# Three transposes of a head in front of the low value products, the shared key's part behind the first pooling projection, and the gains on ACT's queue

## The chip, the cores and the metric

The kernel runs on one core of one Trainium2 chip. The metric is the device time of one execution in microseconds, median of several runs. A core has TensorE (PE: matrix products; PEld is its loading of weights, which overlaps products), VectorE (DVE), ScalarE (ACT), GpSimd (POOL), SyncE (SP, which here only issues DMA transfers) and 16 DMA engines. Products land in PSUM and are taken from there by ACT or VectorE.

## The reference

Two layers of a hybrid trunk over 512 tokens with 16 meta tokens in front (528 columns), model width 1024, everything in float32:

```python
h = rmsnorm(h_res, norm_gain[l])
proj = h @ w_in[l]
u_pool, z_pool, c_q, c_kv, k_rope, z_mla, g_pool, g_mla = jnp.split(proj, IN_SPLIT_POINTS, axis=-1)
y_pool = (pool_mix(u_pool, pool_w_group[l], pool_scale[l]) * jax.nn.silu(z_pool)) @ pool_w_up[l]
o_mla = mla(c_q, c_kv, k_rope, pos, ...)
y_mla = (o_mla * jax.nn.silu(z_mla)) @ mla_w_up[l]
merged = jax.nn.sigmoid(g_pool) * y_pool + jax.nn.sigmoid(g_mla) * y_mla
h_res = h_res + merged @ w_out[l]
```

`pool_mix` is, in four channel groups, a mean over the last 2, 4, 8 or 16 tokens less the token itself, times a 128x128 matrix. `mla` is latent attention with 8 heads: queries from c_q, keys of 64 columns a head and values from c_kv, one rotary key of 32 columns shared by all heads (`k_rope`), RMS norms on queries and keys, causal softmax, values of 64 columns a head. The meta tokens are dropped from the output.

## The kernel before, in words

**Products in three parts.** A float32 product is made of three products in a faster 32-bit format: each operand is split in a high part (ACT copies it in that format, `whi`, `hh`, `th`, `kh`) and a low part (VectorE subtracts the high part, `wlo`, `hl`, `tl`, `kl`), and `mm3` (lines 179 to 182) adds high x high, high x low and low x high. Weights are loaded from memory by SP into `raw` (three buffers), split by `wload` (lines 169 to 177, three buffers), and used.

**The stream.** All weight projections of both layers stand in one list, `plan`: c_q, then for m = 0 to 3 a pooling projection u and a key projection k, the value projection v (`v_body`), the pooling gate and the grouped matrix, the queries, the wide gates and the projections out. A generator, `stream`, issues them product by product; `step`, `fill_now(ns)` and `upto(name)` take as much of it as wanted. The attention is written by hand around it: between its pieces `gap()` takes some 2.9 us of the stream, by a planner's estimate. A scheduler then moves instructions a little on each engine; an engine runs its own in order. `behind(ins, other)` (line 274) makes one instruction wait for another; `newest[0]` is the newest `mm3` product, so that `behind(x, newest[0])` keeps x from its engine's queue until TensorE is there.

**The start.** ACT issues the load of the first weight tile, SP the load of the gains (line 122), x's first block (123), the second weight tile and x's second block. `other_loads` (line 140) issues the rest of x behind the gains' landing. Eight warm-up products on a tile of ones (line 136) run first. `split_h` (line 328) splits x times its gain: high part on ACT, low part on VectorE, the first block in two halves.

**Norms and the shared key.** `norm_sums` sums squares for the two RMS norms and, with `kr_sums`, the shared rotary key (`kp`); the reciprocal roots go through memory and come back as `inv` and `cinv`. `kr_rest` (lines 470 to 480) finishes the shared key in two halves: times `inv` on VectorE (474), a copy on POOL (475), a square and a scaled copy on ACT (477, 479), and `rope`: a shuffle and a product on VectorE (529, 530), a product and a sum on POOL (531, 532). In `go` both halves stand behind `up("u1")`. After them come `columns(1)` (norm factors by token for the values, two small loads on SP), and for groups 0 and 1 `window` (sums on POOL, line 563) and `mix` (VectorE lines 570, 573, 574, then the split, 271 on ACT and 272 on VectorE). u is emptied from PSUM by VectorE (line 540), k by VectorE (628). After c_q's last part `k_factors` (lines 515 to 524) makes the reciprocal roots of the key norms on VectorE (519, then `newton`, 279 to 285), stores them and loads them back spread over all partitions for the first heads (`spread_k`, line 733).

**A head.** `head` makes the scores of four query blocks, their maxima, exponentials and sums; POOL scales the probabilities. `pv` multiplies with the values, for the head before: for each key block j = 0 to 3 it transposes the probability blocks i = j to 3 on TensorE into one PSUM tile (line 839: weights are the probabilities, 128 columns are streamed; 4, 3, 2 and 1 transposes, ten a head), splits the tile into `th` and `tl`, and adds two products to the head's output `o`: high part (line 844, 128 weight columns: value high and low part side by side) and low part (line 845, 64 weight columns). Blocks 0 and 1 stand in the middle of the next head's scores, `pv(prev, (0, 1))` (line 800); 2 and 3 behind the next head's keys and queries, `prep` (line 1066). Behind blocks 0 and 1 of an odd head the probabilities of the meta tokens are transposed (line 850). For the last head, after the loop, o lies in one of the score tiles.

Of the kernel before, what the change touches and what calls it, by code (L numbers as in the profile page):

```python
# [9 lines left out]
F32 = mybir.dt.float32  # L10
F32R = mybir.dt.float32r
# [3 lines left out]
ALU = mybir.AluOpType  # L15
# [39 lines left out]
LAG = 2000.0  # L55
SPL = 240
RET = 12500.0
WARM = 8


def cut(v, bits):
# [10 lines left out]
def trunk(ctx, tc, xT, xrow, mrow, pos, win, wkr, wqb, wkb, wvb, wgr, wpu, wmu, wout, gains, const, yT):  # L72
# [17 lines left out]
    def slot(tag, dt=F32, bufs=1, w=W):  # L90
        return sl.tile([P, w], dt, tag=tag, name=nm(tag), bufs=bufs)
# [27 lines left out]

    early.append(slot("rinv"))  # L120
    act.dma_start(early[0][:, 0:512], win[0, MT_CKV, :, 0:512])
    first = sp.dma_start(gn, gains)
# [43 lines left out]

    loads = [0]

    def wload(src, n, spare):
# [5 lines left out]
        act.activation(hi[:, :n], raw[:, :n], AF.Copy)  # L175
        dve.tensor_sub(lo[:, :n], raw[:, :n], hi[:, :n].bitcast(F32))  # L176
        return hi, lo

    def mm3(out, wh, wl, xh, xl, start, stop):
# [85 lines left out]
    def fill_now(ns):  # L265
        end = clk[0] + ns
        while clk[0] < end and step():
            pass

    def split(hi, lo, src, a, b):  # L270
        act.activation(hi[:, a:b], src, AF.Copy)  # L271
        dve.tensor_sub(lo[:, a:b], src, hi[:, a:b].bitcast(F32))  # L272

    def behind(ins, other):
        tc.add_manual_dep(ins.ins, other.ins.name,
# [33 lines left out]
    class Layer:  # L309
        def __init__(self, l):  # L310
            self.l, self.last = l, l == DEPTH - 1
            self.XS = XTOK if self.last else FULL
            self.x0 = NM if self.last else 0
            self.xt = xt if l == 0 else [None] * 8
            self.hs, self.us, self.zps = hbuf, [None] * 4, [None] * 4
            self.cs, self.cqs, self.ys, self.am = [None] * 2, [None] * 6, [None] * 4, [None] * 8
            self.kn, self.qn, self.zms, self.ogs = [None] * 4, [None] * 4, [None] * 4, [None] * 4
            self.qr, self.qf = [None] * 2, [None] * 2
            self.gms, self.mg, self.xr, self.vw = [None] * 8, [None] * 8, [None] * 8, []
            self.made = [None] * 8  # L320
# [4 lines left out]
        def g(self, c):  # L325
            return gn[:, self.l * N_GAIN + c:self.l * N_GAIN + c + 1]

        def split_h(self, k):
            gk, x = self.g(G_H + k), self.xt[k]
            hh, hl = self.hs[k]  # L330
            for a, b in FULL if (self.l, k) == (0, 0) else [(0, T)]:
                made = act.activation(hh[:, a:b], x[:, a:b], AF.Copy, scale=gk)
                self.made[k] = self.made[k] or made
                dve.scalar_tensor_tensor(out=hl[:, a:b], in0=x[:, a:b], scalar=gk, in1=hh[:, a:b].bitcast(F32),
                                         op0=ALU.mult, op1=ALU.subtract)

        def square_x(self, k):
            self.xsq[k] = slot(f"cq{4 + k}" if k < 4 else f"q{k}")
# [176 lines left out]
        def k_factors(self):  # L515
            flat = lambda d: d.rearrange("h (s c) -> (h s) c", c=T // 16)
            na, ny, nt = (sm.tile([P, T // 16], F32, tag=t, name=nm(t)) for t in ("ka", "ky", "kt"))
            sp.dma_start(na, flat(ksr[self.l]))
            dve.tensor_scalar(na, na, 1.0 / QK, EPS, op0=ALU.mult, op1=ALU.add)
            newton(ny, na, nt)  # L520
            sp.dma_start(flat(kdr[self.l]), ny)
            self.bcs = {}
            for h in range(2):
                self.spread_k(h)
# [234 lines left out]
        def head(self, h, kq, prev):  # L759
# [37 lines left out]
            expo(1, 1, s1, pt[1])  # L797
            expo(2, 2, s2, pt[2])
            self.gap()
            self.pv(prev, (0, 1))  # L800
            self.gap()
            sc = sct()
            s0, s4 = sc[:, 0:144], sc[:, 144:144 + T - SPL]
# [19 lines left out]
        def pv(self, prev, js):  # L823
# [11 lines left out]
            for j in js:  # L835
                n = SEQ - P * j
                tr = mmt()
                for i in range(j, 4):
                    pe.transpose(tr[:, P * (i - j):P * (i - j + 1)], pt[i][:, NM + P * j:NM + P * (j + 1)], ident)  # L839
                th = tp.tile([P, W], F32R, tag="th", name=nm("th"), bufs=2)  # L840
                tl = tp.tile([P, W], F32R, tag="tl", name=nm("tl"), bufs=2)
                split(th, tl, tr[:, :n], 0, n)
                out = ops[:, P * j:512]
                pe.matmul(out, vt[:, j, h, :], th[:, :n], start=j == 0, stop=j == 3)  # L844
                pe.matmul(out[0:64], vt[:, j, h, 0:64], tl[:, :n], start=False, stop=j == 3, skip_group_check=True)  # L845
            if js[-1] != 3:
                if odd == 1:
                    tr = sct() if h == H - 1 else mmt()
                    for i in range(4):
                        pe.matmul(tr[0:64, P * i:P * (i + 1)], self.pmr[:, i].rearrange("p a b -> p (a b)"), identr,  # L850
                                  start=True, stop=True)
                    self.mt = slot("racc", F32R)
                    act.activation(self.mt[0:64, 0:512], tr[0:64, :], AF.Copy)
                    act.activation(self.mt[64:96, 0:512], tr[0:32, :], AF.Copy)
                return
            if odd == 0:
                self.op = tmp()
# [159 lines left out]
        def go(self, nxt):  # L1017
            l = self.l
            up = lambda name: upto((l, name))
            if l == 0:  # L1020
                for k in range(8):
                    if k in (0, 1, 3, 5):
                        step()
                    self.split_h(k)
                    if k == 0:
                        other_loads(first)
# [42 lines left out]
            self.pv(prev, (0, 1))  # L1069
            if not self.last:  # L1070
                self.meta_queries()
            fill_now(2600)
# [88 lines left out]
```

## Time and profile before

| | us |
|---|---|
| median of 3 runs | 783.15 (782.77 to 783.66) |
| the profiled execution | 781.26 |
| its span, first to last instruction | 779.4 |
| TensorE busy | 773.6 (99%) |
| VectorE busy | 535.8 (69%) |
| ACT busy | 413.3 (53%) |
| POOL busy | 205.7 (26%) |

A row of the timeline has the start from the span's start and the duration, both in us, then engine, line, operation, tiles written and read, shapes and count; in brackets the idle time of the engine before it, with what ended it. For a product `128*128 128x264` is rows by weight columns, then what is streamed. In a list of groups the last fields are busy time in us, mean of one in ns, and the engine's idle time ahead of these instructions with what ended it. The row of a stretch gives its ends, its length, then for PE, PEld, DVE, ACT and POOL busy time and count, the granted clock of TensorE, the share of the DMA engines' time and GB/s. The record of a product begins while the one before it still drains, so durations overlap, and starts are compared instead.

### The profile page before, as it was taken

What the parts mean: (1) busy time and instruction counts of PE and PEld (TensorE: products, weight loads), DVE (VectorE), ACT (ScalarE), POOL (GpSimd) and SP (SyncE); (2) the same over time, 40 slices, a digit from 0 to 9 for tenths busy, and PEclk for the clock granted to TensorE, in tenths of its full rate; (3) what the DMA queues carried; (4) which work ended last, traced back from release to release, by engine and by line L of the source; (5) the groups of instructions that cost most, each with busy time, mean ns of one, the idle gap of its engine ahead of it and who ended that gap; (6) DMA issues with size and microseconds to landing.
All of it is one profiled execution on the core that took longest, in us unless ns stands there. A gap on an engine that the chain in (4) does not pass through costs nothing.

```text
span 779.4 us, 14530 instructions
## 1 busy us (share of the span) xinstructions
PE 773.6 (99%) x5251; PEld 703.7 (90%) x5251; DVE 535.8 (69%) x1155; ACT 413.3 (53%) x930; POOL 205.7 (26%) x265
## 2 busy tenths in 40 slices
PE   9999999999999999999999999999999999999998
PEld 9999799999999999999997898887788888888887
DVE  5587788357788977685466467774477888755932
ACT  6754655545565665633354456555445666654420
POOL 1024504012333342043130245130132433420500
PEclk9999999999999999999999999999999999999999
DMA  8533233423222212325642322434242322222372
GB/s 282 164 114 92 74 121 103 116 86 100 91 87 88 82 55 79 95 80 150 186 143 83 109 83 89 132 88 142 69 130 88 96 86 85 62 81 68 106 232 95
DMA packets 54931, 84.04 MB, mean 108 GB/s; under 512 B 10006, under 2 KB 18582, under 8 KB 54860
## 3 DMA queue, kind: packets, MB, share of 16 engines
q1 hardware_dynamic: 54716, 82.86, 34.5%
q8 instruction: 41, 0.67, 0.3%
q14 instruction: 30, 0.25, 0.1%
q10 hardware_dynamic: 144, 0.26, 0.1%
HBM read 76.68 MB, written 4.29 MB: 104 GB/s over the span
## 4 chain that ended last, share of the span: by engine, by line
PE 95%; DVE 2%; ACT 1%; issue 1%; DMA 1%; SPq 0%; DVEq 0%; ACTq 0%
PE mm L180 28%; PE mm L182 27%; PE mm L181 27%; PE mm L839 2%; PE S L180 2%; PE S L181 2%; PE S L182 2%; PE o L844 1%; PE o L845 1%; PE S L498 1%; DVE wlo L176 1%; PE S L462 0%; DMA xb<-xT 0%; DVE tmp L570 0%; PE mm L868 0%
## 5 line engine op out<-in xcount | busy, mean ns | idle before, releaser
L180 PE MATMUL mm<-hh,whi 128*128 128x264 f32 (+2 forms) x1096 | 345.5, 317 | 0.2 <-DVE ky L285 0.2
L181 PE MATMUL mm<-hl,whi 128*128 128x264 f32 (+2 forms) x1096 | 343.2, 314 | 0.0
L182 PE MATMUL mm<-hh,wlo 128*128 128x264 f32 (+2 forms) x1096 | 342.5, 315 | 0.0
L176 DVE TENSOR_TENSOR wlo<-raw,whi 128x512 fp32r<-128x512 f32 (+2 forms) x251 | 185.1, 740 | 107.8 <-ACT whi L175 101.5
L175 ACT ACTIVATE whi<-raw 128x512 fp32r<-128x512 f32 (+2 forms) x251 | 150.5, 602 | 178.5 <-PE mm L181 134.7
L180 PEld LDWEIGHTS mm<-hh,whi 128*128 128x128 f32 x1096 | 205.5, 188 | 13.8 <-issue 0.8
L181 PEld LDWEIGHTS mm<-hl,whi 128*128 128x128 f32 x1096 | 206.1, 188 | 12.0
L182 PEld LDWEIGHTS mm<-hh,wlo 128*128 128x128 f32 x1096 | 205.2, 188 | 12.3
L743 POOL TENSOR_TENSOR tmp<-kp,bc 64x528 f32<-64x528 f32 x16 | 24.8, 1553 | 103.6 <-issue 88.4
L818 POOL TENSOR_TENSOR pm<-pa,rs 128x16 f32<-128x16 f32 x32 | 11.2, 351 | 148.5 <-DVE rs L813 148.5
L604 POOL TENSOR_TENSOR racc<-racc,tmp 128x264 f32<-128x264 f32 (+1 forms) x15 | 14.3, 952 | 112.9 <-ACT tmp L603 112.9
L928 POOL TENSOR_TENSOR tmp<-tmp,xb 128x264 f32<-128x264 f32 (+1 forms) x24 | 26.7, 1134 | 57.7 <-DVE tmp L926 55.5
L774 DVE CUSTOM_DVE_ANT_0 S<-S,maskw,nqs 128x272 f32<-128x272 f32 (+4 forms) x80 | 38.5, 498 | 2.3 <-PE S L182 1.9
L180 PE MATMUL mm<-u,whi 128*128 128x264 f32 (+1 forms) x108 | 35.1, 325 | 0.0
L182 PE MATMUL mm<-u,wlo 128*128 128x264 f32 (+1 forms) x108 | 34.7, 321 | 0.0
L180 PE MATMUL mm<-cq,whi 128*128 128x264 f32 (+1 forms) x108 | 34.6, 320 | 0.0
L182 PE MATMUL mm<-cq,wlo 128*128 128x264 f32 (+1 forms) x108 | 34.5, 321 | 0.0
L181 PE MATMUL mm<-cq,whi 128*128 128x264 f32 (+1 forms) x108 | 34.5, 321 | 0.0
L272 DVE TENSOR_TENSOR tl<-mm,th 128x512 fp32r<-128x512 f32 (+1 forms) x64 | 29.3, 482 | 6.8 <-ACT th L271 5.7
L781 ACT ACTIVATE cq<-S,bia 128x400 f32<-128x400 f32 (+2 forms) x48 | 24.5, 515 | 17.8 <-DVE bia L808 8.8
L820 POOL TENSOR_TENSOR cq<-cq,rs 128x384 f32<-128x384 f32 (+1 forms) x32 | 33.5, 1047 | 0.0
L271 ACT ACTIVATE th<-mm 128x512 fp32r<-128x512 f32 (+1 forms) x64 | 25.4, 434 | 6.5 <-PE mm L839 5.9
(271 smaller groups left out, 1370.9 us busy)
## 6 DMA issues: line engine op xcount, KB each, us to landing
raw<-win SPq DMA_DIRECT2D x143, 256.0 KB, 2.6
raw<-wout SPq DMA_DIRECT2D x32, 256.0 KB, 3.1
bc<-kdr SPq DMA_DIRECT2D x16, 264.0 KB, 3.3
raw<-wpu SPq DMA_DIRECT2D x16, 256.0 KB, 2.7
raw<-wmu SPq DMA_DIRECT2D x16, 256.0 KB, 2.7
raw<-wqb SPq DMA_DIRECT2D x12, 256.0 KB, 2.9
xb<-xT SPq DMA_DIRECT2D x8, 264.0 KB, 4.5
tmp<-xT SPq DMA_DIRECT2D x16, 132.0 KB, 3.0
```

What stands on the lines that cost most here:

```text
L175: act.activation(hi[:, :n], raw[:, :n], AF.Copy)
L176: dve.tensor_sub(lo[:, :n], raw[:, :n], hi[:, :n].bitcast(F32))
L180: pe.matmul(out, wh, xh, start=start, stop=False)
L181: pe.matmul(out, wh, xl, start=False, stop=False)
L182: newest[0] = pe.matmul(out, wl, xh, start=False, stop=stop)
L271: act.activation(hi[:, a:b], src, AF.Copy)
L272: dve.tensor_sub(lo[:, a:b], src, hi[:, a:b].bitcast(F32))
L743: gp.tensor_mul(kf[r0:r0 + 64, :], self.kp[r0:r0 + 64, :], bc[r0:r0 + 64, :])]
L774: dve.tensor_tensor_reduce(out=sv, in0=sv, in1=mask, scale=nqs[:, i, h:h + 1], scalar=3e38, op0=ALU.add, op1=ALU.min, accum_out=bia[:, c:c ...
L781: act.activation(pv, sv, AF.Exp, scale=-1.0, bias=bia[:, i:i + 1], accum_out=rs[:, c:c + 1])
L820: gp.tensor_mul(pt[i][:, NM:], pt[i][:, NM:], rs[:, i:i + 1].to_broadcast([P, n - NM]))
L928: gp.tensor_add(t[:, :b - a], t[:, :b - a], self.am[m][:, a:b])
```

## The change

- **Transposes.** `pv` is called three times for a head: with (0,) where (0, 1) stood, with (1,) a gap after the scores' end, ahead of `prep`, and with (2, 3) one gap later. (0,) makes only the seven transposes of blocks 0 and 1 and splits them. (1,) makes the products of blocks 0 and 1: the first product waits for its split's low part, then come a transpose of block 2, half of the low product (256 columns), the other transpose of block 2, the other half; then block 1's first product, block 3's transpose, and block 1's low product. Blocks 2 and 3 share one PSUM tile and one split of 384 columns. (2, 3) makes their products. An order-only dependency (`follow`) keeps each triple together. For the last head, after the loop, all three transposes stand together ahead of the products.
- **Start.** The gains' load goes from SP's queue to ACT's, behind the first weight tile's. The rest of x waits for ACT's first activation (the warm-up copy). The high part of x's first half block is made by VectorE; the order of the first splits and weight splits is set by `held`. Seven warm-up products.
- **Shared key.** `kr_rest` stands behind `up("u0")`, each half after `fill_now(1300)`, and `up("u1")` follows.
- **Key norms.** The first step of `k_factors` on VectorE waits for the newest product.

```diff
-    first = sp.dma_start(gn, gains)
+    act.dma_start(gn, gains)
...
-    act.activation(warm, warm, AF.Copy)
+    first = act.activation(warm, warm, AF.Copy)
...
+                if (self.l, k, a) == (0, 0, 0):
+                    made = dve.tensor_scalar(hh[:, a:b], x[:, a:b], gk, None, op0=ALU.mult)
+                else:
+                    made = act.activation(hh[:, a:b], x[:, a:b], AF.Copy, scale=gk)
...
-            dve.tensor_scalar(na, na, 1.0 / QK, EPS, op0=ALU.mult, op1=ALU.add)
+            behind(dve.tensor_scalar(na, na, 1.0 / QK, EPS, op0=ALU.mult, op1=ALU.add), newest[0])
...
+            def product(j, c, th, tl, made, cuts=1, between=()):
+                n = SEQ - P * j
+                out = ops[:, P * j:512]
+                last = pe.matmul(out, vt[:, j, h, :], th[:, c:c + n], start=j == 0, stop=j == 3)
+                if between:
+                    behind(last, made)
+                for k in range(cuts):
+                    if between:
+                        t = turn(*between[k])
+                        follow(t, last)
+                        last = t
+                    a, b = n // cuts * k, n // cuts * (k + 1)
+                    mm = pe.matmul(out[0:64, a:b], vt[:, j, h, 0:64], tl[:, c + a:c + b], start=False, stop=j == 3,
+                                   skip_group_check=True)
+                    if between:
+                        follow(mm, last)
+                    last = mm
...
+            elif js[0] == 1:
+                t2 = mmt()
+                product(0, 0, *self.t01[0], cuts=2, between=((t2, 0, 2, 2), (t2, P, 3, 2)))
+                product(1, 0, *self.t01[1], between=((t2, 2 * P, 3, 3),))
+                self.t23 = parts(t2, 384)
...
+            up("u0")
+            for a, b in FULL:
+                fill_now(1300)
+                self.kr_rest(a, b)
             up("u1")
-            for a, b in FULL:
-                self.kr_rest(a, b)
-                fill_now(1300)
...
                 kn_ = self.head(h, kq, prev)
                 self.gap()
+                self.pv(prev, (1,))
                 if h + 1 < H:
                     kq = self.prep(h + 1)
+                self.gap()
                 self.pv(prev, (2, 3))
                 prev = kn_
-                self.gap()
```

More of the change, by code (lines that the diff above doesn't have):

```diff
@@ L57 @@
 RET = 12500.0
-WARM = 8
+WARM = 7
 def cut(v, bits):
@@ L167, in trunk @@
     loads = [0]
+    held = [None]
     def wload(src, n, spare):
@@ L174, in wload @@
         lo = pool.tile([P, W if pool is tp else 512], F32R, tag=tl, name=nm("wlo"), bufs=nb)
-        act.activation(hi[:, :n], raw[:, :n], AF.Copy)
-        dve.tensor_sub(lo[:, :n], raw[:, :n], hi[:, :n].bitcast(F32))
+        made = [act.activation(hi[:, :n], raw[:, :n], AF.Copy),
+                dve.tensor_sub(lo[:, :n], raw[:, :n], hi[:, :n].bitcast(F32))]
+        for ins, other in zip(made, held[0] or ()):
+            if other is not None:
+                behind(ins, other)
+        held[0] = None
         return hi, lo
@@ L834, in pv, with turn, parts @@
                 dve.tensor_sub(self.pmr[:, :, 1, :], pm, self.pmr[:, :, 0, :].bitcast(F32))
[L835 to L839, printed above, removed]
+            def turn(tr, c, i, j):
+                return pe.transpose(tr[:, c:c + P], pt[i][:, NM + P * j:NM + P * (j + 1)], ident)
+            def parts(tr, n):
@@ L840, in pv @@
                 th = tp.tile([P, W], F32R, tag="th", name=nm("th"), bufs=2)
                 tl = tp.tile([P, W], F32R, tag="tl", name=nm("tl"), bufs=2)
-                split(th, tl, tr[:, :n], 0, n)
+                return th, tl, split(th, tl, tr[:, :n], 0, n)
+            def product(j, c, th, tl, made, cuts=1, between=()):
+                n = SEQ - P * j
                 out = ops[:, P * j:512]
-                pe.matmul(out, vt[:, j, h, :], th[:, :n], start=j == 0, stop=j == 3)
-                pe.matmul(out[0:64], vt[:, j, h, 0:64], tl[:, :n], start=False, stop=j == 3, skip_group_check=True)
@@ L1020, in go @@
             if l == 0:
-                for k in range(8):
-                    if k in (0, 1, 3, 5):
+                held[0] = None, self.split_h(0, FULL[:1])[1]
+                step()
+                held[0] = self.split_h(0, FULL[1:])
+                other_loads(first)
+                for k in range(1, 8):
+                    if k in (1, 3, 5):
                         step()
                     self.split_h(k)
-                    if k == 0:
-                        other_loads(first)
             if l:
```

56 lines of the change are left out of this document (38 added, 18 removed).

## The prediction

> **What bounds the kernel now.** I read the page first, then the products by shape with what they waited for, then the timeline of each place where TensorE stood still.
>
> ```profile
> span 779.4 us, 14530 instructions
> PE 773.6 (99%) x5251; PEld 703.7 (90%) x5251; DVE 535.8 (69%) x1155; ACT 413.3 (53%) x930; POOL 205.7 (26%) x265
> PE 95%; DVE 2%; ACT 1%; issue 1%; DMA 1%; SPq 0%; DVEq 0%; ACTq 0%
> L180 PE MATMUL mm<-whi,kh 128*128 128x512 f32 x16 | 6.5, 415 | 1.3 <-DVE u L540 1.2
> ```
>
> TensorE carries 95% of the chain that ended last, and it is busy 99% of the span, so time is won only by making its slots shorter or by closing the few places where it waits. Of its waits inside the run, most belongs to one line: the value projection of layer 0 and 1 (stationary kh, moving whi), held by VectorE's line 540. That group shows 1.3 us. The timeline shows more, because a wait also spoils the overlap of the next products:
>
> ```profile
> 78.73 0.28 PE L182 MATMUL mm<-kh,wlo 128*128 128x264 f32 x1
> 79.97 0.47 PE L180 MATMUL mm<-whi,kh 128*128 128x512 f32 x1 [0.95 <-DVE u L540]
> ...
> 81.70 0.39 PE L181 MATMUL mm<-wlo,kh 128*128 128x512 f32 x1
> ...
> 77.01 1.50 DVE L176 TENSOR_TENSOR wlo<-raw,whi 128x512 fp32r<-128x512 f32 x1
> 78.43 1.05 DVE L574 TENSOR_TENSOR tmp<-tmp,u 128x16 f32<-128x16 f32 x1
> 80.88 0.43 DVE L540 TENSOR_TENSOR u<-mm,rinv 128x264 f32<-128x264 f32 x1
> ...
> 78.04 1.41 POOL L563 TENSOR_TENSOR tmp<-tmp 128x540 f32<-128x540 f32 x1
> ```
>
> The product that starts at 79.97 waits for a PSUM tile that line 540 (eviction of u3) has still to empty. VectorE is late there: a weight split takes 1.50 us and a 16-column subtraction 1.05 us, both while POOL runs a window sum (77 to 79.4 us). Those are pieces of the pooling mixer of groups 0 to 2, and they are that late because the shared key's part (kr_rest, lines 474 to 532) went through VectorE and POOL just ahead of them.
>
> ```profile
> 100.48 0.19 DVE L284 TENSOR_TENSOR kt<-kt,ka 128x33 f32<-128x33 f32 x1
> 101.20 0.42 DVE L549 SCALAR_TENSOR_TENSOR xb<-mm,rinv 128x264 f32<-128x264 f32 x1
> ...
> 101.25 0.28 PE L182 MATMUL mm<-u,wlo 128*128 128x264 f32 x1
> 101.77 0.36 PE L180 MATMUL mm<-hh,whi 128*128 128x264 f32 x1 [0.24 <-DVE ky L285]
> ...
> 470.57 1.38 DVE L272 TENSOR_TENSOR tl<-tmp,u 128x512 fp32r<-128x512 f32 x1
> ...
> 471.91 0.28 PE L182 MATMUL mm<-kh,wlo 128*128 128x264 f32 x1
> 472.44 0.47 PE L180 MATMUL mm<-whi,kh 128*128 128x512 f32 x1 [0.24 <-DVE u L540]
> ```
>
> At 101 us it is the reciprocal root of the key norms (lines 519 and 279 to 285), whose small steps stand in VectorE's queue between evictions. At 471 us it is layer 1's copy of the first place, with a mixer split of 1.38 us in front of the eviction.
>
> **The unit of the sum: what a product costs.** A product's record overlaps the next one, so I use the step from one start to the next.
>
> ```profile
> 193.85 0.76 PE mm L839 x7
> ...
> 239.07 0.28 PE L180 MATMUL mm<-hh,whi 128*128 128x264 f32 x1
> 239.19 0.27 PE L839 MATMUL mm<-cst,cq 128*128 128x128 f32 x1
> ...
> 239.42 0.29 PE L182 MATMUL mm<-hh,wlo 128*128 128x264 f32 x1
> ...
> 662.03 0.34 PE L844 MATMUL o<-th,vt 128*128 128x384 f32 x1
> 662.21 0.27 PE L839 MATMUL mm<-cst,cq 128*128 128x128 f32 x1
> 662.23 0.42 PE L845 MATMUL o<-tl,vt 128*64 128x384 f32 x1
> 662.49 0.40 PE L182 MATMUL mm<-hh,wlo 128*128 128x512 f32 x1
> 662.73 0.40 PE L180 MATMUL mm<-hh,whi 128*128 128x512 f32 x1
> ```
>
> 264 columns take 0.12 us (239.07 to 239.19), 384 take 0.18 (662.03 to 662.21), 512 take 0.24 (662.49 to 662.73). A transpose in a row of transposes takes 0.76/7 = 0.11. A lone one in front of a product with 128 weight columns: 239.19 to 239.42 is 0.23 for both, less 0.12, again 0.11.
>
> **The transposes.** The change takes 3 of 10 transposes out of their rows and puts them in front of second (low-part) value products, whose weights have 64 columns. In the built order of the changed kernel that holds for 7 of 8 heads in both layers: 14 x 3 = 42 transposes, always first product, transpose, low product. The kernel before happens to have exactly this once: at 662.03 first product, transpose, low product. Transpose and low product take 662.21 to 662.49 = 0.28; the low product alone should take the 0.18 of its 384 columns. So the transpose costs 0.10 here too, against 0.11 in the row. I take a gain of 42 x 0.005, 0.2 us, and call it nothing. Bounds: 0.02 us (the rounding of two starts) either way, 42 x 0.02 = 0.8 us lost or won.
>
> [...]
>
> The first low product is cut in two, 14 times:
>
> ```profile
> L845 PE MATMUL o<-tl,vt 128*64 128x512 f32 x14 | 5.6, 400 | 0.0
> L845 PE MATMUL o<-tl,vt 128*64 128x256 f32 x14 | 3.9, 280 | 0.0
> ```
>
> Of a 512-column record of 0.40 the step is 0.24, so 0.16 overlaps the next; for 256 columns 0.28 - 0.16 = 0.12, twice 0.24. The cut costs nothing, to 0.02 x 14 = 0.3 us. One eviction a head goes away (j = 2 and 3 share a tile): ACT and VectorE time, at 53% and 69%, with no wait of TensorE on it. It frees nothing on the path. The products come a gap later; nothing reads the head's output sooner than the mixer projections after head 7.
>
> **Shared key's part earlier.** kr_rest moves from behind u1 to behind u0. Its work is the same (per layer two multiplications and two rotary chains on VectorE, six operations on POOL, four on ACT, no DMA); what moves forward by about one u and one k projection, 7 us, is the mixer of groups 0 and 1 behind it. In the built order the four small mixer steps and both mixer splits of these groups now all stand ahead of u3's evictions; around those stand only weight splits and key evictions. The excess in layer 0 is 81.70 - 78.73 = 2.97 for one step of 0.12 and five of 0.24 (1.32), so 1.65 us. I take 1.4 of it as won. Bounds: nothing (another late eviction takes its place) and 1.65. In layer 1: 472.44 - 471.91 = 0.53 less 0.12, 0.4 us; I take 0.3, bounds 0 and 0.4. The column scales that follow it on SP's queue (lines 432, 433) go one weight load earlier; they are small.
>
> **The key norms' root later.** It now waits for the newest product after cq5, and stands some sixty instructions later in VectorE's queue, among the rotary queries, whose PSUM ACT empties and not VectorE. The place at 101 us loses its cause: 101.77 - 101.25 = 0.52 less 0.12, 0.4 us, of which I take 0.3 (bounds 0 and 0.4). Price where it lands: the store and the three broadcast loads stand in SP's queue in front of weight loads:
>
> ```profile
> 101.75 0.33 SPq L521 DMA_DIRECT2D kdr<-ky  x1
> 103.44 1.28 SPq L733 DMA_DIRECT2D bc<-kdr  x3
> ```
>
> SP stands 101.75 to 103.44 for the store, and 3 us in all until weights go on. Before, that hid behind weights loaded ahead and TensorE did not wait at 104 us. In the new place weights are two or three ahead too. I take 0.1 us lost, bounds 0 and 1.5 (half the stand, in one layer).
>
> **The start.**
>
> ```profile
> 0.74 0.39 SPq L122 DMA_DIRECT2D gn<-gains  x1
> 1.18 3.15 DMA xb<-xT
> 3.67 0.63 ACT L175 ACTIVATE whi<-rinv 128x512 fp32r<-128x512 f32 x1 [1.00 <-DMA rinv<-win]
> 4.43 0.92 ACT L332 ACTIVATE hh<-xb,gn 128x264 fp32r<-128x264 f32 x2
> 4.99 0.69 PEld L180 LDWEIGHTS S<-hh,whi 128*128 128x128 f32 x2 [0.45 <-ACT hh L332]
> 5.61 0.63 ACT L175 ACTIVATE whi<-raw 128x512 fp32r<-128x512 f32 x1 [0.26 <-DMA raw<-win]
> ...
> 4.99:6.30 1.31, 1.31 (x5) 1.01 (x5) 0.91 (x4) 0.99 (x2) 0.00 (x0) 1.00 1.06 366
> ```
>
> With the gains on ACT's queue, x's first block is issued 1.18 - 0.74 = 0.44 us sooner, and VectorE makes hh while ACT makes whi, so the first product can go when whi is done, 3.67 + 0.63 = 4.3 against 4.99; the eighth warm-up product is dropped for it. (The further loads of x wait for ACT's first activation now and not for the gains.) But the next product needs the second weight (5.61), and the DMA engines are full by then (share 1.06), so that comes only as much sooner as the stream starts sooner. I take 0.3 us; bounds 0 (the gains, second in ACT's queue, land late) and 0.7.
>
> **The sum.** 0.3 (start) + 1.4 + 0.3 (value projections) + 0.3 (at 101 us) - 0.1 (root's new place) + 0 (transposes, cut) = 2.2 us. The profiled execution took 781.26 (779.4 of span and 1.9 around it), so 779.1. The median of the runs shown is 783.15, 1.9 above it; I take the same difference off: **780.9 us**.
>
> **The rivals.**
> [...]
> - *The waits only move.* The mixer's pieces come earlier, collide with POOL there, and u2's evictions or the second value weight hold TensorE instead; half of the 2.0 us is kept and the start gives nothing: 783.15 - 1.0 + 0.1 = 782.2, no change. [...] Against: VectorE idles before 62 us. Chance 0.22.
> - *The locked order stands.* First product, transpose and low product are tied; the first product now waits for the low part as well, and TensorE runs in order, so a late VectorE stops everything behind it, 14 times. The cover is the gap of other products in between (60 products, 7 us, in the first head). It decides against the change from 2.2/14 = 0.16 us each; at 0.3 each, 4.2 us, it gives 785.1. For it: VectorE is at 69%. Against: the length of the gap. Chance 0.13.
> - *The change doesn't do what it says*: the scheduler could have torn the triples apart; the built order shows them whole, so no chance is given.
>
> **How the numbers follow.** The forecast has 0.53, with its own range 779.9 to 781.6 (start 0.7 and everything closed, or two of the four terms halved). A measurement of this kernel tells 0.2%, 1.6 us, from no change. Faster: 0.53 + 0.12 = 0.65; within: 0.22; slower: 0.13. The range reaches down to the first rival and up past the second, to where the third begins: 778.5 to 783.4.
>
> **What would show it.** Right: the first value product following the last key product without a wait in both layers; no stop at zp's first product; first real product near 4.4 us; transpose and low product of 384 columns still 0.28 together, of 256 columns 0.23. Wrong: that pair at 0.23, or TensorE idle in front of the first value product of a head, on the low split.

## The result, and the profile after

| | before | after |
|---|---|---|
| median, us | 781.44 (780.93 to 783.66, 14 runs) | 784.60 (782.67 to 785.77, 14 runs) |
| ratio | | 1.0038 (95%: 1.003 to 1.0045) |
| span of the profiled execution, us | 779.4 | 782.4 |

The change costs 3.2 us; forecast was a gain of 2.2. (The three runs shown ahead of the prediction, 783.15, lay 1.7 above the median of all 14. The forecast time carried that along, which by luck makes the miss look smaller: 3.7 us in the time, 5.4 in the change.) The page after:

```profile
span 782.4 us, 14483 instructions
PE 92%; DVE 4%; DMA 1%; ACT 1%; issue 1%; POOL 0%; ACTq 0%; POOLq 0%
```

The chain that ended last (by engine) has 92% of TensorE where it had 95%, and VectorE's share has doubled to 4%. The groups of products by shape say where TensorE stood:

```profile
L186 PE MATMUL mm<-whi,kh 128*128 128x512 f32 x16 | 6.0, 395 | 0.0
L186 PE MATMUL S<-kh,qhl 128*128 128x272 f32 x16 | 4.9, 309 | 1.9 <-ACT cq L793 1.9
L186 PE MATMUL S<-hh,whi 128*128 128x264 f32 x16 | 4.8, 331 | 1.6 <-ACT hh L344 1.6
L186 PE MATMUL mm<-hh,whi 128*128 128x264 f32 x784 | 224.0, 288 | 0.7 <-ACT whi L177 0.7
L859 PE MATMUL o<-th,vt 128*128 128x512 f32 x14 | 5.5, 395 | 0.0
```

The 1.3 us of the value projections are gone, as forecast. Three new waits have come: 1.6 us at the first real product, 0.7 at 59 us, 1.9 at the scores of one head.

To see what each is worth I laid the trace against that of before by the number of columns that TensorE had streamed in products (the warm-ups left out), and took the difference of the starts. Each row is one execution, the profiled one. Numbers in us at the place that the kernel before reaches at that time; positive is late:

| place in before | 10 | 60 | 90 | 110 | 280 | 300 | 480 | 760 |
|---|---|---|---|---|---|---|---|---|
| changed kernel | 2.00 | 2.94 | 1.25 | 0.78 | 1.08 | 3.58 | 3.37 | 2.99 |

So 2.0 us are lost before 10 us and 0.9 at 59; the value projections and the place at 101 give back 2.2; one stop between 280 and 300 loses 2.5.

**The start.** The timeline of the changed kernel:

```profile
1.05 3.35 PE L136 MATMUL wps<-ones 128*128 128x128 f32 x14 [1.05 <-DVE na L731]
...
4.56 0.63 ACT L177 ACTIVATE whi<-rinv 128x512 fp32r<-128x512 f32 x1 [1.40 <-DMA rinv<-win]
5.53 0.51 ACT L344 ACTIVATE hh<-xb,gn 128x264 fp32r<-128x264 f32 x1 [0.34 <-DMA gn<-gains]
6.05 0.78 PE L186 MATMUL S<-hh,whi 128*128 128x264 f32 x2 [1.64 <-ACT hh L344]
...
7.36 0.42 PE L186 MATMUL mm<-hh,whi 128*128 128x264 f32 x1
7.58 0.42 PE L187 MATMUL S<-hl,whi 128*128 128x264 f32 x1
```

The gains are there only at 5.53 and the first weights at 4.56 (before: 3.67). TensorE's warm-ups end at 4.40, so it stands 1.64 us. Then a product of 264 columns steps by 0.22 us (7.36 to 7.58) and not by 0.12. That is the step that the start alone shows where the trace has the granted clock at 0.50 (9.05 to 9.27); it is called the low clock here. By stretches of 3.41 us, first the kernel before, then the changed one (length, then busy time and count of PE, PEld, DVE, ACT, POOL, the clock where the trace has a record of it, DMA share, GB/s):

```profile
2.89:6.30 3.41, 3.25 (x15) 2.67 (x13) 1.56 (x4) 2.18 (x4) 0.77 (x5) 1.00 1.04 369
6.30:9.71 3.41, 3.41 (x27) 3.33 (x27) 2.91 (x5) 2.97 (x5) 0.00 (x0) 1.00 0.95 320
```

```profile
3.46:6.88 3.42, 1.78 (x9) 1.51 (x8) 1.30 (x4) 1.95 (x4) 0.24 (x4) 1.00 1.06 395
6.88:10.29 3.41, 3.41 (x17) 3.41 (x17) 3.41 (x6) 2.22 (x4) 0.00 (x0) 1.00 0.93 307
```

The trace's record of the raised clock begins at 6.30 before and at 10.29 after; the column of the clock reads 1.00 ahead of that too, since there is no record yet, so read the counts: 17 products in the stretch from 6.88 against 27 in the one from 6.30. TensorE was busy for 1.78 of 3.42 us in the stretch ahead.

**The stop in a head.** Layer 0, between 280 and 300 us in the table:

```profile
287.68 0.39 PE L186 MATMUL S<-kh,qhl 128*128 128x272 f32 x1 [1.91 <-ACT cq L793]
...
282.06 0.77 DVE L846 TENSOR_TENSOR pmr<-pm,pmr 128x128 fp32r<-128x128 f32 x1 [2.16 <-ACT pmr L845]
282.85 1.75 DVE L754 TENSOR_TENSOR tmp<-kn,bc 64x528 f32<-64x528 f32 x1
284.62 0.51 DVE L786 CUSTOM_DVE_ANT_0 S<-S,maskw,nqs 128x272 f32<-128x272 f32 x1
...
281.72 0.31 ACT L845 ACTIVATE pmr<-pm 128x128 fp32r<-128x128 f32 x1 [1.96 <-POOL pm L830]
...
286.94 0.59 ACT L793 ACTIVATE cq<-S,bia 128x400 f32<-128x400 f32 x1
...
281.47 0.21 POOL L830 TENSOR_TENSOR pm<-cq,rs 128x16 f32<-128x16 f32 x1
...
282.65 1.38 POOL L755 TENSOR_TENSOR tmp<-kp,bc 64x528 f32<-64x528 f32 x1
```

Read it from the end. The scores of head 7 (287.68) need the PSUM tiles of head 6's scores, which the exponential at 286.94 empties. That waits for the maxima (line 786, from 284.62), and these for nothing but their place in VectorE's queue (the row of 284.62 has no wait of its own): ahead of them stand the low part of the meta probabilities (282.06), which waits by ACT for POOL's last scaling (281.47), and the key product of prep(7) (282.85), which takes 1.75 us beside POOL's. In the kernel before two of the three maxima stood ahead of both.

### The profile page after: what moved, and what is told of

It reads as the page before. It is cut to its first block, busy times and chain, and to the rows that moved or that the text cites. A ratio compares the mean times of both kernels' runs of the same rounds, so it can differ in the third digit from the quotient of the medians.

```text
span 782.4 us, 14483 instructions
## 1 busy us (share of the span) xinstructions
PE 773.5 (99%) x5263; PEld 705.2 (90%) x5263; DVE 534.7 (68%) x1140; ACT 410.5 (52%) x913; POOL 204.2 (26%) x265
## 4 chain that ended last, share of the span: by engine, by line
PE 92%; DVE 4%; DMA 1%; ACT 1%; issue 1%; POOL 0%; ACTq 0%; POOLq 0%
PE mm L186 27%; PE mm L187 27%; PE mm L188 27%; PE mm L849 2%; PE S L187 2%; PE S L188 1%; PE S L186 1%; PE o L868 1%; PE o L859 1%; DVE wlo L178 1%; PE S L510 1%; DMA raw<-wout 1%; DVE S L786 1%; DMA gn<-gains 1%; DVE tmp L754 1%
## 5 line engine op out<-in xcount | busy, mean ns | idle before, releaser
L178 DVE TENSOR_TENSOR wlo<-raw,whi 128x512 fp32r<-128x512 f32 (+2 forms) x251 | 187.8, 751 | 117.1 <-ACT whi L177 113.5
L786 DVE CUSTOM_DVE_ANT_0 S<-S,maskw,nqs 128x400 f32<-128x400 f32 (+4 forms) x80 | 38.6, 498 | 1.1 <-PE S L188 0.7
L832 POOL TENSOR_TENSOR cq<-cq,rs 128x384 f32<-128x384 f32 (+1 forms) x32 | 31.8, 994 | 0.0
L278 DVE TENSOR_TENSOR tl<-mm,th 128x384 fp32r<-128x384 f32 (+1 forms) x46 | 26.8, 594 | 5.9 <-ACT th L277 5.7
L187 PE MATMUL mm<-kn,whi 128*128 128x264 f32 (+1 forms) x88 | 28.4, 324 | 0.0
```

Of the source, the lines that this page charges most:

```text
L187: pe.matmul(out, wh, xl, start=False, stop=False)
L278: return dve.tensor_sub(lo[:, a:b], src, hi[:, a:b].bitcast(F32))
L786: dve.tensor_tensor_reduce(out=sv, in0=sv, in1=mask, scale=nqs[:, i, h:h + 1], scalar=3e38, op0=ALU.add, op1=ALU.min, accum_out=bia[:, c:c ...
L832: gp.tensor_mul(pt[i][:, NM:], pt[i][:, NM:], rs[:, i:i + 1].to_broadcast([P, n - NM]))
```

## The experiments

Offsets as in the table above, of all kernels that the argument rests on; medians beside those of the kernel before on the same chip; the ratio is that to the kernel before:

| kernel | median (before) | ratio, 95% | 10 | 60 | 90 | 110 | 280 | 300 | 480 | 760 |
|---|---|---|---|---|---|---|---|---|---|---|
| start alone | 784.04 (781.16) | 1.0021 to 1.0043 | 2.28 | 2.97 | 2.94 | 3.05 | 3.01 | 3.01 | 3.04 | 3.05 |
| shared key alone | 778.25 (781.16) | 0.9946 to 0.9971 | -0.24 | -0.24 | -1.93 | -2.41 | -2.48 | -2.48 | -2.99 | -3.02 |
| transposes alone | 784.04 (781.16) | 1.0021 to 1.0047 | -0.44 | -0.43 | -0.47 | -0.45 | -0.13 | 2.38 | 2.49 | 2.13 |
| changed, start as before | 782.71 (781.16) | 1.0005 to 1.0022 | 1.59 | 1.65 | -0.05 | -0.52 | -0.22 | 3.62 | 3.04 | 2.65 |
| transposes, maxima first | 781.10 (781.21) | 0.9991 to 1.0008 | -0.13 | -0.13 | -0.16 | -0.15 | -0.37 | 0.03 | -0.08 | -0.46 |
| start, 12 warm-ups | 784.67 (781.21) | 1.0031 to 1.0058 | 0.87 | 1.53 | 1.50 | 2.83 | 2.82 | 2.82 | 3.09 | 3.07 |
| the same, meta row first | 783.94 (781.11) | 1.0022 to 1.0047 | 0.81 | 0.93 | 0.93 | 2.40 | 2.41 | 2.41 | 2.93 | 2.95 |
| start, gains first | 784.14 (781.23) | 1.0026 to 1.0054 | 1.52 | 2.74 | 2.73 | 2.86 | 2.86 | 2.87 | 2.88 | 2.87 |
| the same, meta row first | 784.00 (781.23) | 1.0022 to 1.0047 | 2.23 | 3.68 | 3.66 | 3.78 | 3.86 | 3.88 | 3.86 | 3.88 |
| changed, start as before, maxima first | 778.24 (781.11) | 0.9951 to 0.9976 | -0.47 | -0.46 | -2.15 | -2.62 | -2.91 | -2.49 | -3.17 | -3.54 |
| changed, three mends | 779.52 (781.11) | 0.9970 to 0.9988 | 0.92 | 1.02 | -0.67 | -1.14 | -1.40 | -1.02 | -1.70 | -2.02 |

**The parts, one by one.** Each is the kernel before with one part of the diff; the fourth is the changed kernel without the start's part.

> The kernel before with the start alone changed (gains on ACT's queue, first high part on VectorE, order of the first splits, seven warm-up products). Theory 1, the start costs by itself: the first real product comes at 6.05 us instead of 4.99 and the clock is raised near 10.3 us instead of 6.3, as in the changed kernel, and the 1.54 us that the changed kernel is behind at 28 us stay to the end or shrink to no less than 1.0: 782.4 to 783.1, 1.0 to 1.6 over the kernel before (781.4). Rival, the weights' stream hides it: the delay is gone by 60 us, within 0.3 of the kernel before.

> The kernel before with the shared key's part behind u0 and the key norms' wait alone. Theory 1: the three value stalls close as in the changed kernel (1.65 + 0.4 + 0.4) and the late first eviction of u at 58.8 us does not appear, since it comes from the late start: 2.0 to 2.4 us faster, 779.0 to 779.5. Rival, the late eviction belongs to this part: TensorE stands 0.7 to 0.9 us near 57 us, and 1.0 to 1.6 are left, 779.9 to 780.4.

> The kernel before with the transposes and the value products a gap later alone. Theory 1: the stop of 2.07 us in head 5 of layer 0, before the scores that wait for the exponentials, belongs to the new order of the attention and comes back: 2.4 to 3.2 us slower, 783.8 to 784.6. Rival, the stop is an accident of the time at which POOL and VectorE met in the changed kernel: no stop over 0.5 us in the heads, and within 0.7 of the kernel before, 780.7 to 782.1.

> The changed kernel with the start as before. Theory 1: the first product is back at 4.99 us and the clock at 6.3, the eviction at 58.8 us is in time or late by less than 0.4, and the rest is as in the changed kernel: 1.3 to 2.3 us faster than it, 782.2 to 783.3. Rival, the head's stop is an accident of timing and goes with the 1.5 us: 779 to 780.5.

Measured: +2.9, -2.9, +2.9 (sum +2.9 against 3.2 for the whole), and +1.6 without the start (its two parts sum to 0). The shared key's part wins by itself what the whole change was forecast to win, and more. The start costs twice the 1.0 to 1.6 expected: the 1.54 us read at 28 us match the delay of one store on SP's queue (29.77 against 28.23), while TensorE is 2.3 us late at 10 us in the start alone. It has the late eviction at 58 us, too (2.32 to 2.97 between 50 and 60 us); the shared key's part has not. The head's stop comes with the transposes alone.

The fourth run was meant to have an undisturbed start, but 8 warm-ups do not secure that: its first weights came at 4.14 us instead of 3.67 and it lost 1.59 us in the first ten. It shows a second price, of the stop. By stretches of 3.41 us:

```profile
279.55:282.97 3.42, 3.42 (x31) 3.42 (x30) 2.20 (x2) 1.43 (x3) 3.17 (x4) 1.00 0.22 77
282.97:286.38 3.41, 1.51 (x14) 1.37 (x13) 3.36 (x11) 1.95 (x6) 0.00 (x0) 1.00 0.00 0
286.38:289.80 3.42, 3.42 (x14) 3.26 (x15) 3.42 (x9) 2.12 (x5) 0.00 (x0) 0.50 0.24 77
```

TensorE was busy 1.51 us of one stretch, and in the next the granted clock was 0.50, with 14 products instead of 31. The stop cost 3.8 us in this execution (-0.22 to 3.62), against 2.5 with the transposes alone (-0.13 to 2.38), where the trace has 24 products and a clock of 1.00 from 286.38 to 289.80. The profiled execution is the slowest of the twelve, but in ten of them the mean granted clock is 0.997 or 0.998, and the two at 0.999 are the fastest (781.18 and 781.50). By an estimate, 3.42 us at 0.50 take 0.002 off the mean of a span of 782 us, so most executions of this kernel likely had such a stretch.

**The head's stop.** Kernel "transposes alone", and VectorE's two instructions put behind the third maximum:

```diff
-            top(2, 2, s2, causal(400))
+            self.topped = top(2, 2, s2, causal(400))
...
-                dve.tensor_sub(self.pmr[:, :, 1, :], pm, self.pmr[:, :, 0, :].bitcast(F32))
+                behind(dve.tensor_sub(self.pmr[:, :, 1, :], pm, self.pmr[:, :, 0, :].bitcast(F32)), self.topped)
...
+            else:
+                behind(made[0], self.topped)
```

> The kernel before with the transposes' part alone, and in every head VectorE's low part of the meta probabilities (pmr) and its key product of prep stand behind the third maximum of the head's first scores. Theory: the stop in head 6 of layer 0 comes from these two standing ahead of all three maxima while VectorE waits for POOL; the maxima then come at about 279 us, the exponentials near 282, and the stop of 1.93 us is gone: 781.2 to 782.2, that is 1.8 to 2.8 less than the same part without it. Rival, POOL's scaling is late anyway and the scores' buffers come free no sooner: 783.3 or more.

Measured 781.10, 2.9 less. VectorE in that place:

```profile
278.53 0.51 DVE L780 CUSTOM_DVE_ANT_0 S<-S,maskw,nqs 128x272 f32<-128x272 f32 x1 [0.66 <-PE S L182]
...
282.87 0.27 DVE L840 TENSOR_TENSOR pmr<-pm,pmr 128x128 fp32r<-128x128 f32 x1
283.15 0.70 DVE L746 TENSOR_TENSOR tmp<-kn,bc 64x528 f32<-64x528 f32 x1
```

The first maximum waits for its scores alone, the key product no longer meets POOL's and takes 0.70 instead of 1.75, and TensorE does not stop. So the whole loss of the transposes' part was this order (how much of it is the place in the queue and how much the 1.75 us beside POOL, no run parts). With it mended the part is worth nothing against the kernel before: the interval holds 1.

**The start's clock.**

```diff
-WARM = 7
+WARM = 12
```

> The kernel before with the start alone changed, but twelve warm-up products instead of seven. Theory, the clock: what costs is that TensorE stands still for 1.6 us after the warm-ups, so that the raised clock is given late or taken back for 3.4 us; with the hole filled it stays raised from about 5.6 us, and 1.5 to 1.9 us come back, 782.0 to 782.7 (the late data and the late eviction at 58 us stay). Rival, the late gains are the cost by themselves: 783.7 or more.

> The kernel before with seven warm-up products instead of eight, nothing else. Theory, the clock: TensorE then stands 0.58 us instead of 0.16 ahead of the first real product, and most executions get the raised clock only near 10 us: a median of 782.5 to 783.2. Rival, the missing warm-up product costs nothing since the data set the start: 780.9 to 781.5 as the kernel before.

> The kernel before with the shared key's part alone and nine warm-up products. Theory, the clock: the warm-ups end at 5.3 us at the low clock and cover the landing of the first weights, also in executions where it is late; the median stays where it was or rises by no more than 0.3 (778.0 to 778.6), and no execution lies over 779.2. Rival, the ninth product only delays the first real one and everything behind: 778.6 to 779.0.

With twelve warm-ups the hole is closed and the offset at 10 us falls from 2.28 to 0.87: 1.4 us of the start's loss there were hole and clock, 0.9 are left to the data. (The 1.9 and 0.5 in expectations below come from a count that takes the warm-ups' columns for work done.) The median did not follow (784.67): 0.6 are lost at 58 us, and 1.3 more between 90 and 110. The expectation, 782.0 to 782.7, was wrong in that.

The kernel before with seven warm-ups had the median of the kernel before (781.18 against 781.21): wrong as well. In its profiled execution TensorE stood 0.86 us of the stretch from 4.02 to 7.43 and had 29 products in the 3.42 us behind it; but 3 of its 11 executions took 782.4 to 783.0, and none of 21 of the kernel before beside it over 781.5 (of 19 beside the first four kernels 3 did, at 782.9 to 783.1). None of those was profiled. Short idle time went both ways in the profiles: 0.86 us here, with 16 products in the stretch that has it, and 0.66 us in the changed kernel with the start as before, with 17 products at steps of 0.22 us from 6.49 to 9.90. In all five profiles with a hole of 1.56 to 1.78 us (the changed kernel, the start alone, the gains waited for, the gains first, and the same with the meta row first) products of 264 columns then step by 0.22 us. The ninth warm-up of the shared key's kernel neither cost nor won (778.11).

**The norms' order.** What else is late with the start? SP's stores of the sums of squares (nsr) and the load of all of them (nq), before and with the start alone:

```profile
28.23 0.62 SPq L401 DMA_DIRECT2D nsr<-tmp  x1
28.96 0.61 SPq L366 DMA_DIRECT2D nsr<-sx  x1
31.94 0.39 SPq L365 DMA_DIRECT2D nsr<-sx  x1
35.07 0.33 SPq L409 DMA_DIRECT2D nq<-nsr  x1
```

```profile
30.07 0.61 SPq L409 DMA_DIRECT2D nsr<-tmp  x1
33.77 0.39 SPq L373 DMA_DIRECT2D nsr<-sx  x1
34.76 0.62 SPq L374 DMA_DIRECT2D nsr<-sx  x1
39.29 0.34 SPq L417 DMA_DIRECT2D nq<-nsr  x1
```

The first store is 1.84 us late, the load 4.22. The store of the meta tokens' sums (line 366, then 374) has changed places with that of the tokens' sums: with the start's other timing the scheduler squares the meta row last. The changed kernel has the same order. So I restored that order on top of the twelve warm-ups:

```diff
-                    r, src = (P, xrow[:, k]) if k < 8 else (2 * NM, mrow)
+                if i == 10:
+                    meta = slot("bc", bufs=3)[0:2 * NM, 0:512]
+                    behind(sp.dma_start(meta, mrow), newest[0])
...
+                if i == 18:
+                    behind(act.activation(meta, meta, AF.Square, accum_out=sx[0:2 * NM, 0, 4:5]), newest[0])
```

> The changed start alone with twelve warm-up products, and ACT squares the meta tokens' row before the last row of tokens, as the kernel before does (so that their small store goes out before the last store and not behind it). Theory: with the clock mended only 0.5 us of late data are left at 10 us; the rest of the loss (0.65 at 58 us, 1.3 between 90 and 110 us) comes from the norms, which this swapped order makes 2.2 us later than the start does; so the load of the sums goes out near 35.7 us instead of 37.8 and 781.4 to 782.4 are left. Rival, the norms are late because of the late data, and the order has no part in it: 783.8 or more, as with twelve warm-up products alone.

The load goes out at 36.12 (37.82 without), and the loss at 58 us is nearly gone (the offset at 60 us is 0.93 instead of 1.53). The median falls by 0.7 only (the intervals overlap), to 783.94 where 781.4 to 782.4 were expected: the larger loss, at 101 us, is there with this order and without it (1.47 and 1.33 between 90 and 110):

```profile
91.46 0.33 SPq L531 DMA_DIRECT2D ka<-ksr  x1
94.51 0.18 DVE L532 TENSOR_SCALAR ka<-ka 128x33 f32<-128x33 f32 x1 [3.79 <-DMA ka<-ksr]
...
104.17 0.36 PE L186 MATMUL mm<-hh,whi 128*128 128x264 f32 x1 [1.71 <-DVE ky L291]
```

VectorE stands 3.79 us for the load of the key sums, and TensorE 1.71 instead of the 0.24 of before. The load lands 3.0 us after its issue (2.9 with twelve warm-ups alone), where it took 1.6 in the kernel before and 1.7 with the start alone; what makes it slower is not shown. That is the place that the change's other part, the wait for the newest product, clears; with the start alone it is open, and what the warm-ups win at 10 us is lost there.

**Why the data are late.**

> The changed start alone, but the rest of x's loads waits for the gains' landing again, as before. Theory, the queue: the gains land late because they stand behind the 256 KB of the first weights on ACT's queue, so keeping the other loads away helps little; first real product at 5.5 us or later, and 783.3 or more. Rival, the crowd: the other loads, released at 3.2 us, share the DMA engines with the gains; without them the gains are there by 4.5 us, the first real product comes by 5.1, and 782.0 or less.

> The changed start alone, with the gains' load issued on ACT's queue ahead of the first weights' load instead of behind it. Theory, the place in the queue: the gains are there before the weights, the first real product comes at 4.6 to 5.3 us (when the first weights are split), TensorE stands for less than 1 us after its seven warm-up products, and the clock's loss is gone in most executions; the swapped order of the norms stays, with its 0.6 us at 58 us and a later stop at 101: 781.6 to 783.0. Rival, the gains are late because x's first block now shares the engines from 0.74 us on: first real product at 5.6 us or later, 783.4 or more.

> As the kernel with the gains first, and the meta tokens' row squared before the last row of tokens. Theory, late gains and the swapped order are all that the start costs: within 0.6 of the kernel before, 780.6 to 781.7. Rival, something else in the new start (the first weights landing later beside x's block, or the order of the first splits) costs too: 782.2 or more.

> The changed start alone, but the second weights' and the second x block's loads (issued at 1.19 and 1.65 us) go out only when the gains have landed, so that the first weights, the gains and x's first block have the DMA engines to themselves. Theory, the crowd: the first weights are split from 3.9 us or sooner instead of 4.6, the gains are used by 4.0 to 4.3 and the first real product comes by 4.9. Rival, ACT's queue moves the gains only behind the weights' 256 KB whatever else runs: the gains are used at 5.0 us or later. The whole time is no test, since the second weights come later: 782.5 to 785.

The four edits, each on the start alone: the rest of x waits for the gains' landing; the gains ahead of the first weights on ACT's queue; the same with the meta row first; and the second weights and x's second block kept back until the gains have landed.

```diff
-    first = act.activation(warm, warm, AF.Copy)
+    act.activation(warm, warm, AF.Copy)
-    act.dma_start(gn, gains)
+    first = act.dma_start(gn, gains)
```

```diff
+    act.dma_start(gn, gains)
     act.dma_start(early[0][:, 0:512], win[0, MT_CKV, :, 0:512])
-    act.dma_start(gn, gains)
```

```diff
-    early.append(fetch(win[0, MT_CKV + 1, :, 0:512], 512, rawt(), sp))
-    sp.dma_start(xb[:, 1, :T], xT[:, 1, :])
+    early.append(rawt())
+    behind(sp.dma_start(early[1], win[0, MT_CKV + 1, :, 0:512]), landed)
+    behind(sp.dma_start(xb[:, 1, :T], xT[:, 1, :]), landed)
```

The rest of x's loads is not it: gains at 5.53 and first product at 6.05, as in the changed kernel (5.66 and 6.18 with the start alone), 783.62. With the gains first:

```profile
3.69 0.52 ACT L340 ACTIVATE hh<-xb,gn 128x264 fp32r<-128x264 f32 x1 [0.53 <-DMA gn<-gains]
5.29 0.63 ACT L177 ACTIVATE whi<-rinv 128x512 fp32r<-128x512 f32 x1 [1.08 <-DMA rinv<-win]
5.97 0.59 PE L186 MATMUL S<-hh,whi 128*128 128x264 f32 x1 [1.56 <-ACT whi L177]
```

the gains come 1.84 us sooner than in the changed kernel and the weights 0.73 later, the first product hardly sooner (5.97 against 6.05), and the time is the same (784.14; 784.00 with the meta row first). Both expectations failed. With the meta row first the place at 58 us is not cleared here: its profiled execution, the slowest of its five, loses 1.4 us between 50 and 60 us (2.24 to 3.68), and 0.9 are lost without that edit (1.84 to 2.74). So the swapped order alone does not make the late eviction; what else does is open. With the second weights and second x block kept back, gains are used at 4.81 instead of 5.53, but the weights still come at 4.55:

```profile
0.74 0.39 SPq L127 DMA_DIRECT2D xb<-xT  x1
0.74 0.41 ACTq L125 DMA_DIRECT2D rinv<-win  x1
...
4.55 0.63 ACT L182 ACTIVATE whi<-rinv 128x512 fp32r<-128x512 f32 x1 [1.39 <-DMA rinv<-win]
4.81 0.36 DVE L339 TENSOR_SCALAR hh<-xb,gn 128x264 fp32r<-128x264 f32 x1 [3.79 <-DMA gn<-gains]
```

(787.51, above the expected range: the second weights then come late, three later blocks of x go out ahead of them, at 3.18, and the mean granted clock of the profiled execution is 0.996, with 0.8 in the first fortieth of its span.) Shown is this, against the changed kernel: whichever of the two stands second on ACT's queue is there only after 5.2 us while the other loads run; the place in the queue is worth 1.84 us to the gains, keeping two loads back 0.72. That the weights come at 4.55 even then, 0.9 later than in the kernel before, leaves x's first block, issued in the same instant (0.74) and not 0.44 later, as the likely cause. The gains' load close behind on the same queue is a rival, no run moved either alone, and with the old start the weights came at 4.14 in one profile.

**The mends together.**

> The changed kernel with the start as before and VectorE's low part of the meta probabilities and key product behind the third maximum. Theory: nothing but the value stalls is changed in time, and they close: 777.8 to 778.6, as with the shared key's part alone. Rival, the parts disturb each other (the key product, held back, makes the next head's keys late): 779.5 or more.

> The changed kernel, all parts kept, with three mends: twelve warm-up products, the meta tokens' row squared before the last row, and the maxima ahead of pmr and the key product. Theory, three causes and no more: 784.6 less 1.9 (clock) less 1.3 to 1.9 (norms) less 2.0 to 2.5 (stop in head 6): 778.3 to 779.4. Rival, one of the mends fails in company: 780.5 or more.

The shared key's part with the mended transposes and the old start takes 778.24, as much as the shared key's part alone (778.25): the transposes' part brings nothing in company either. The changed kernel with all its parts and three mends takes 779.52, 1.6 less than the kernel before, where without them it takes 3.2 more; the upper end of the expectation was 779.4. What it lacks to 778.24 is the start: its offset at 10 us is 0.92, the other's -0.47. The version to keep is the shared key's part alone.

## Why the prediction was wrong

- **The start, -0.3 forecast, +2.9 alone: the step that failed most.** The step "the first product can go when whi is done, 3.67 + 0.63 = 4.3" took the weights' landing from the profile of before and left it where it was, though two transfers were issued 0.44 us sooner beside it. The weights came at 4.56, the gains at 5.53, and the first product went at 6.05. The bound that I named, "the gains, second in ACT's queue, land late", was priced at nothing. It costs a hole of 1.64 us, and behind the hole come 3.41 us at the low clock, with 17 products where the kernel before has 27 (together 1.4 of 2.3 us at 10 us, by twelve warm-ups; 0.9 are the late data). Seven warm-ups end at 4.40, eight at 4.84, so the one dropped makes the hole longer.
- **The order behind the start.** A different start changed the scheduler's order of the norms' last squares. The late eviction at 58 us (0.65) was in no term. Restoring the order cleared it with twelve warm-ups, but not with the gains first, so its cause is shown in part.
- **The transposes, 0 forecast: right for the transposes, wrong for the part.** The triples in the changed kernel:

```profile
220.33 0.27 PE L849 MATMUL mm<-cst,cq 128*128 128x128 f32 x1
220.36 0.36 PE L868 MATMUL o<-tl,vt 128*64 128x256 f32 x1
220.56 0.27 PE L849 MATMUL mm<-cst,cq 128*128 128x128 f32 x1
...
220.96 0.27 PE L849 MATMUL mm<-cst,cq 128*128 128x128 f32 x1
220.99 0.42 PE L868 MATMUL o<-tl,vt 128*64 128x384 f32 x1
221.24 0.29 PE L186 MATMUL mm<-hh,whi 128*128 128x264 f32 x1
```

  Transpose and low product take 0.23 together with 256 columns (220.33 to 220.56) and 0.28 with 384 (220.96 to 221.24), the marks that were set. The 0.12 in the chances and the range's lower end, 778.5, stand for a gain of 2.3 us by the transposes. No run shows one: the pair of 384 columns costs its 0.28 in both kernels, and with the maxima first the part took 781.10 against 781.21. What failed is the step "The products come a gap later; nothing reads the head's output sooner than the mixer projections after head 7", which put the new order at nothing and cost the 2.5 us stop: I looked for who reads the output, not for what the moved calls of `pv` and `prep` do to the maxima in VectorE's queue. The built order shows it in the head's line: pmr, key product, three maxima.
- **The locked order.** Its 785.1 is nearest to the result, and for the wrong reason: no first product of a head waited for the low split (the group of 512 columns above has no idle time).
- **The shared key, -1.9 forecast (1.4 + 0.3 + 0.3 - 0.1), -2.9 alone: right, and too small.** The row that released the value product at 79.97 in the kernel before is the first eviction of u3; the one at 80.88 that the prediction shows came after it, and ended the second wait, of the weights loaded at 81.36:

```profile
79.41 0.42 DVE L540 TENSOR_TENSOR u<-mm,rinv 128x264 f32<-128x264 f32 x1
```

  In the changed kernel the first value product follows with no wait:

```profile
81.68 0.29 PE L188 MATMUL mm<-kh,wlo 128*128 128x264 f32 x1
81.81 0.40 PE L186 MATMUL mm<-whi,kh 128*128 128x512 f32 x1
```

  The offsets of the part alone give 1.69 in layer 0 (-0.24 to -1.93), 0.48 at 101 us, 0.51 between 300 and 480 us: the whole excess of each place and a little more, where I took off a fifth. Another 0.24 stand at 10 us, ahead of anything that this part changes, and are not its gain; what brought them is not shown. The root's new place cost nothing.
- **"The waits only move"** was the right suspicion, for the wrong part: with the start alone, what twelve warm-ups won at 10 us was lost again at 101 us.

## What to carry to other kernels

Price a moved transfer by what it shares the engines with from its new instant on, and check when the product that needs it can then start; with the start alone a hole of 1.78 us ahead of it was followed by 3.42 us at a clock of 0.50 besides. When a part of a program is moved under a scheduler, read the built order of the engines that it does not name: the loss in the head here was two instructions that came to stand ahead of the maxima in VectorE's queue, and a dependency (`behind`) on each took it away. Try the parts of a change singly; here one part of three carried all of the gain.

## What the runs showed of the hardware

- With the start alone products of 264 columns step by 0.12 us from 7.25 to 7.37, by 0.22 from 9.05 to 9.27, and by 0.12 again from 11.63 to 11.75; the granted clock is 0.50 from 8.12 to 11.54, for 3.42 us:

```profile
4.71:8.12 3.41, 1.94 (x12) 1.65 (x12) 2.41 (x6) 3.00 (x6) 0.00 (x0) 1.00 1.03 376
8.12:11.54 3.42, 3.42 (x18) 3.36 (x17) 3.42 (x7) 2.79 (x5) 0.00 (x0) 0.50 0.93 332
```

  The stretch ahead of that one had TensorE busy for 1.94 us: the hole of 1.78 us, from 4.40 to 6.18, reaches into it. In the changed kernel with the start as before a stretch busy for 1.51 us, with 1.90 idle, was followed by 3.42 us at 0.50, with 14 products. With the transposes alone TensorE was busy for 1.58 us from 282.97 to 286.38, and the 3.42 us behind had 24 products at 1.00.
- So the stop in the head cost 2.5 us in one execution and 3.8 in the other. What decides between the two is not shown.
- A key product on VectorE took 1.75 us beside POOL's, and 0.70 by itself.
